# A decoder step in float32: scores, values and state products of the sample tokens on four column groups of TensorE instead of two

## The chip, the cores and the metric

One Trainium2 chip, one core of it. The metric is the device time of the kernel in microseconds (us), as the median of several runs. Before the change three runs took 1352.76, 1353.05 and 1354.18 us, so the median is 1353.05.

## What is computed

One inference step of a hybrid decoder layer, for a prompt of 1024 tokens and for 32 sample tokens (8 batches of 4). One input projection feeds three branches (a gated MLP, a Mamba-2 scan, a cross-attention to 256 memory tokens), one output projection joins them. The change touches the sample tokens alone, in two places. Each of the 8 batches has its own keys, values and scan state:

```python
y_off = jnp.einsum('bclgn,bcgkpn,bclgk->bclgkp', cm, h_prev, jnp.exp(acum))   # C times the state, 16 heads x 64
s = jnp.einsum('bthd,bmhd->bhtm', qh, mem_k) * (MEM_HEAD_DIM ** -0.5)         # 4 heads x 256
p = jax.nn.softmax(s, axis=-1)
o = jnp.einsum('bhtm,bmhd->bthd', p, mem_v)
```

## The kernel before

**The main line.** TensorE does large projections all the time. `gemmA` and `gemmB` run eight k-steps of three matmuls each (lines 290 to 292 in `gemm3`): the operands are split into a float32r part and its remainder. One call is a block; `spill` makes three blocks of 352 tokens from one weight unit, each block is evicted by ScalarE into a tile `gt` (line 701) and stored by a DMA on the SyncE queue (line 702, `mg_d<-gt` and the like).

**The side work.** The sample tokens are handled by a generator, `side_chain()`, stepped from `hook()` after each k-step. The pace is 0.43, so one step of the generator falls after every two or three k-steps, and a bare `yield` is a step without work that lets other engines finish. The generator runs `sample_scan` and then `sample_att` beside the projections; `side.drain()` runs what is left when the projections of that part are through. TensorE takes all of it in program order.

**Products with the states** (`sample_scan`, `s1` and `s2`). Per batch b: `s1` transposes the state (0.5 MB, tile `hb`, line 1027) into `hTb`; `s2(b, 0)` multiplies it by the masked C. The stationary operand has 32 columns, so the product uses 32 of the array's 128 columns. Group g of the heads goes to the column group that starts at column 32 g (`tile_position`), 512 columns of states streaming: two products per batch (line 1039), accumulated over the batches in one PSUM bank. After the last batch two copies of 32x512 take the sums out (line 1070).

**Scores** (`sample_att`). Keys come as 32 half tiles `kv` of 0.5 MB (16 of keys, 16 of values; half a holds heads 2a and 2a+1), five buffers. Per batch and half there is one step of eight transposes (line 1152, copied by ScalarE and VectorE into `kTb`, two buffers) and, one half later, one step of scores: two parts of the head dimension times two heads, four products of 32 stationary and 256 streaming columns, head h on column group h (line 1137). This makes 16 score steps.

**Values.** After the softmax the probabilities are spread into the mask tile `pm`. Per batch and half: a load of the half that comes four later (line 1117), and four products, two halves of the memory times two heads (line 1188). This makes 16 value steps.

**The queue.** All these DMAs are issued by SyncE in program order. A load of `kv` waits until TensorE has read the buffer that it overwrites; a store `mg_d<-gt` waits for ScalarE's eviction. What stands behind a waiting DMA waits too.

Of the kernel before, what the change touches and what calls it, by code (L numbers as in the profile page):

```python
# [58 lines left out]
def hybrid_step(ctx, tc, x_prompt, x_sample, mem_prompt, state_ssm, state_conv, cache_mem_k,  # L59
# [25 lines left out]
    # every float32 operand of the large products is split exactly into a float32r part (H) and  # L85
    # a float32r remainder (L); products are H*H + H*L + L*H, accumulated in float32
# [17 lines left out]
    def split(raw, H, L, heng, leng):  # L104
        """H = float32r(raw), L = raw - H"""
        if heng is ACT:
            ACT.activation(out=H, in_=raw, func=AF.Copy)  # L107
        else:
            heng.tensor_copy(out=H, in_=raw)
        leng.tensor_tensor(out=L, in0=raw, in1=rb(H), op=ALU.subtract)  # L110

# [114 lines left out]
    # 1 where the token belongs to the batch: 0 <= p - 4 b <= 3  # L226
# [17 lines left out]
    class RowNorm:  # L244
        """rows xt [T, 1024] -> dH + dL [128, 8, T] = (rmsnorm(xt) * g)^T"""
# [27 lines left out]
    # work that runs beside the large products: stepped between their parts  # L273
# [12 lines left out]
    def gemm3(ps, lhs, rhs, k0, kn, first, last, mid=None):  # L286
        """ps += sum over k of lhs(k)^T rhs(k) in three float32r products"""
        for k in range(k0, k0 + kn):
            (lH, lL), (rH, rL) = lhs(k), rhs(k)
            PE.matmul(out=ps, lhsT=lH, rhs=rH, start=(first and k == k0), stop=False)  # L290
            PE.matmul(out=ps, lhsT=lH, rhs=rL, start=False, stop=False)  # L291
            PE.matmul(out=ps, lhsT=lL, rhs=rH, start=False, stop=(last and k == k0 + kn - 1))  # L292
            if mid is not None and k == 3:
                mid()
            hook()
# [10 lines left out]
    def gemmA(w, mH, mL, t0, n):  # L306
        """weights stationary: [128 channels, n tokens]"""
        ps = mm()
        gemm3(ps[:, :n], lambda k: (w[0][:, k, :], w[1][:, k, :]),
              lambda k: (mH[:, k, t0:t0 + n], mL[:, k, t0:t0 + n]), 0, KD, True, True)  # L310
        w_tick()
        return ps

    def gemmS(wp, n, dst):
        """the 32 sample tokens stationary, H and L side by side: [dst = 32 tokens, n channels]; the weights
        are released"""
        ps = mm()
        for k in range(KD):
            wH, wL = wp[k // 4][0][:, k % 4, :], wp[k // 4][1][:, k % 4, :]
            if k > 0:  # L320
                PE.matmul(out=ps[:32, :n], lhsT=xS[:, k, 0:32], rhs=wL, start=False, stop=False)
            PE.matmul(out=ps[:64, :n], lhsT=xS[:, k, :], rhs=wH, start=(k == 0), stop=(k == KD - 1))
            if k == 0:
                PE.matmul(out=ps[:32, :n], lhsT=xS[:, k, 0:32], rhs=wL, start=False, stop=False)
            if k == 3:
                w_half()
            hook()
        w_done(1)
        ACT.activation(out=dst, in_=ps[:32, :n], func=AF.Copy)
        DVE.tensor_tensor(out=dst, in0=dst, in1=ps[32:64, :n], op=ALU.add)  # L330
        w_tick()

    def gemmB(mH, mL, t0, T, wp, n, last=False):
        """tokens stationary: [T tokens, n channels]; after the last tile the weights are released"""
        ps = mm()
        gemm3(ps[:T, :n], lambda k: (mH[:, k, t0:t0 + T], mL[:, k, t0:t0 + T]),
              lambda k: (wp[k // 4][0][:, k % 4, :], wp[k // 4][1][:, k % 4, :]), 0, KD, True, True,
              w_half if last else None)
        if last:
            w_done(1)  # L340
        w_tick()
        return ps

    # =====================================================================
    # Phase B: Mamba-2
    # =====================================================================
# [48 lines left out]
    # the activation table is loaded while the first rows arrive  # L395
# [15 lines left out]
    def setup_side():  # L411
# [5 lines left out]
        # conv state, transposed  # L417
# [7 lines left out]
        # rows of the decay products: rows 0-7 and 8-15 pick a head (1 on its columns), 16-17 hold  # L425
        # the running sums (H, L) of the chunk
# [52 lines left out]
    # parameter vectors, one 128-vector per row, then transposed  # L479
# [22 lines left out]
    def x_side(t):  # L502
        # beside the products of tile t: transposes of tile t + 1, norm of tile t + 2
# [31 lines left out]
    def dt_chain(pool):  # L535
# [10 lines left out]
        # log1p(e) = ln(u) * e / (u - 1), or e where u == 1  # L546
# [9 lines left out]
        # dta = -exp(a_log) * dt  # L556
# [53 lines left out]
    def chunk_rows(i0):  # L610
        """rows of chunk i % 8 of group i // 8, four of them"""
# [104 lines left out]
    def gate_norm(pool, y, sz, T):  # L716
        """y = y * sz; returns the scale to unit mean square; y, sz [T, 512]; sz is overwritten"""
# [29 lines left out]
    def lr_copy(i):  # L747
        """decay rows of chunks i .. i + 3"""
        if i < 16:
            DVE.tensor_copy(out=Lt, in_=Lraw)  # L750
            DVE.tensor_copy(out=Rt, in_=Rraw)
            if i + 4 < 16:
                chunk_rows(i + 4)
# [34 lines left out]
    def sC(i):  # L788
        """the chunk's C, for the product with the state"""
# [11 lines left out]
    def sE(i, j):  # L801
        """masked decays of four heads (transposed): exp(min(diff, 0))"""
# [137 lines left out]
    def sample_scan(sp2):  # L940
# [39 lines left out]
        # H, L, H of B against H, H, L of x: one pass over 96 rows  # L980
# [54 lines left out]
        def s2(b, j):  # L1035
            hbt, hTb, Bm = St[b]
            if j == 0:
                for g in range(2):
                    PE.matmul(out=accs[32 * g:32 * g + 32, :], lhsT=Cm[:, g, b * 32:(b + 1) * 32],
                              rhs=hTb[:, g * 512:(g + 1) * 512], start=(b == 0), stop=(b == 7), tile_position=(0, 32 * g))  # L1040
# [23 lines left out]
        for g in range(2):  # L1064
# [5 lines left out]
            DVE.tensor_copy(out=t1[:, cs], in_=accs[32 * g:32 * g + 32, :])  # L1070
# [21 lines left out]
    def softmax_rows(pool, ps, n):  # L1092
        """ps [128, n, 256] scores -> P [128, n, 256]"""
# [15 lines left out]
    def sample_att(sap):  # L1109
# [23 lines left out]
        def scores(b, a):  # L1133
            kTb = kTs.pop((b, a))
            for dt in range(2):
                for h in (2 * a, 2 * a + 1):
                    PE.matmul(out=psS[h * 32:(h + 1) * 32, :], lhsT=qm[:, 2 * h + dt, b * 32:(b + 1) * 32],
                              rhs=kTb[:, 2 * (h - 2 * a) + dt, :], start=(b == 0 and dt == 0), stop=(b == 7 and dt == 1),
                              tile_position=(0, h * 32))

        prev = None
        for b in range(8):
            for a in range(2):
                kv_load()
                kb = kvq.pop(0)
                kTb = sap.tile([128, 4, 256], F32, tag="kTb", name="kTb", bufs=2)
# [13 lines left out]
                if prev is not None:  # L1160
                    scores(*prev)
                    yield
                prev = (b, a)
        yield
        scores(*prev)
# [16 lines left out]
        for b in range(8):  # L1182
            for a in range(2):
                kv_load()
                vb = kvq.pop(0)
                for m in range(2):
                    for h in (2 * a, 2 * a + 1):
                        PE.matmul(out=psO[h * 32:(h + 1) * 32, :], lhsT=pm[:, m, h, b * 32:(b + 1) * 32],
                                  rhs=vb[:, m, (h - 2 * a) * 256:(h - 2 * a + 1) * 256], start=(b == 0 and m == 0),
                                  stop=(b == 7 and m == 1), tile_position=(0, h * 32))  # L1190
# [36 lines left out]
    # =====================================================================  # L1227
    # Phase A: spatial-gating MLP
    # =====================================================================
# [90 lines left out]
    def mix(h):  # L1320
        """mixes head h; the result takes the place of v: vt[:, c, h] = [channels, tokens of chunk c]"""
# [52 lines left out]
    TB = [(0, 384), (384, 384), (768, 288)]  # L1374

    def outproj(H, L, first, at=None):
        units = [(ct, b) for ct in range(8) for b in range(3)]
        if first:
            # the last tokens are split last
# [35 lines left out]
    def splitA(c, leng=DVE):  # L1415
        """all heads of token tile c"""
# [53 lines left out]
    # =====================================================================  # L1470
    # Phase C: memory cross-attention
    # =====================================================================
# [27 lines left out]
    n = 0  # L1500
# [140 lines left out]
    def y_load(i):  # L1641
        """summed output of the other branches: the block's tokens of one channel tile"""
# [23 lines left out]
    # the output weights stay: the first ones in the slots of the stream  # L1666
# [20 lines left out]
    def rows_part(b, ct):  # L1687
        """transposes of one channel tile back to token rows, plus the residual"""
# [15 lines left out]
        if ct in SQE:  # L1704
# [12 lines left out]
            # the gain, once the squares are taken  # L1717
# [91 lines left out]
```

## Time and profile before

| what | number |
|---|---|
| median of three runs | 1353.05 us |
| profiled execution, first to last instruction (its span) | 1351.7 us |
| TensorE busy (matmul) | 1320.8 us, 98% |
| VectorE, ScalarE, GpSimd busy | 590.4, 496.5, 210.4 us |
| scan of the sample tokens, its products with states | about 516 to 562 us of the span |
| scores of the sample tokens | about 590 to 655 us |
| values of the sample tokens | about 662 to 698 us |

The rows come from one profiled execution; its device time isn't listed by itself, so the span (1351.7) stands for it, 1.35 us below the median of the runs. In the profile, a float32 product of the sample tokens shows as two MATMUL records: 64 products of scores are 128 records. A float32r matmul, and a transpose, is one record. [...]

### The profile page before, as it was taken

Reading aid. Unit: us, or ns where it says so; the run is one execution under the profiler, and the core shown is the slowest. Engines: PE = TensorE matmul, PEld = TensorE weight load, DVE = VectorE, ACT = ScalarE, POOL = GpSimd, SP = SyncE. Lnnn points to the kernel's source line nnn. Section 1 sums busy time; section 2 is a strip of 40 time slices with the busy share of each in tenths; the row PEclk is TensorE's granted clock in tenths of the full one; section 3 lists DMA queues with packets and bytes.
Section 4 is the critical chain, followed back from the end, with each engine's and each line's share of the span. In section 5 each row is a group of like instructions: output and inputs, shape, how many; then the busy total and the mean of one; then the engine's idle time right before and its main releaser. Section 6 shows DMA issues by size and latency. Waiting matters only on the chain. (4 is left out here: it accounts for less than half of the span.)

```text
span 1351.7 us, 22582 instructions
## 1 busy us (share of the span) xinstructions
PE 1320.8 (98%) x9231; PEld 1236.4 (91%) x9231; DVE 590.4 (44%) x943; ACT 496.5 (37%) x962; POOL 210.4 (16%) x274
## 2 busy tenths in 40 slices
PE   8999999999999999999999999999999889999996
PEld 7999999988888898888779999998999889999996
DVE  6212545566767632422112245345312646654543
ACT  6323444464545432222211124344313633322322
POOL 4200000043434424200000010002000600000122
PEclk9999999999999999999999999999999999999999
DMA  6223111122222245475551114221423565436432
GB/s 223 78 77 99 44 48 48 47 88 76 78 72 88 82 118 165 149 226 179 181 181 45 32 32 127 68 68 44 144 93 128 177 178 182 151 117 193 139 121 95
DMA packets 171595, 151.44 MB, mean 112 GB/s; under 512 B 13781, under 2 KB 155049, under 8 KB 171493
## 3 DMA queue, kind: packets, MB, share of 16 engines
q1 hardware_dynamic: 171492, 150.01, 36.1%
q8 instruction: 72, 1.18, 0.4%
q14 instruction: 31, 0.25, 0.1%
HBM read 111.97 MB, written 37.79 MB: 111 GB/s over the span
## 5 line engine op out<-in xcount | busy, mean ns | idle before, releaser
L290 PE MATMUL ps_mm<-xH,wh 128*128 128x352 f32 x1056 | 359.9, 341 | 0.0
L292 PE MATMUL ps_mm<-xH,wl 128*128 128x352 f32 x1056 | 339.6, 322 | 0.0
L291 PE MATMUL ps_mm<-xL,wh 128*128 128x352 f32 x1056 | 339.2, 321 | 0.0
L290 PEld LDWEIGHTS ps_mm<-xH,wh 128*128 128x128 f32 x1056 | 198.3, 188 | 25.3 <-issue 21.0
L291 PEld LDWEIGHTS ps_mm<-xL,wh 128*128 128x128 f32 x1056 | 199.0, 188 | 0.7
L292 PEld LDWEIGHTS ps_mm<-xH,wl 128*128 128x128 f32 x1056 | 198.4, 188 | 0.0
L110 DVE TENSOR_TENSOR wl<-wr,wh 128x1024 fp32r<-128x1024 f32 (+2 forms) x106 | 121.8, 1161 | 175.2 <-ACT wh L107 174.8
L290 PE MATMUL ps_mm<-wh,xH 128*128 128x256 f32 (+1 forms) x512 | 148.0, 289 | 0.0
L291 PE MATMUL ps_mm<-wl,xH 128*128 128x256 f32 (+1 forms) x512 | 146.4, 286 | 0.1
L292 PE MATMUL ps_mm<-wh,xL 128*128 128x256 f32 (+1 forms) x512 | 145.6, 284 | 0.3 <-DVE xL L110 0.3
L107 ACT ACTIVATE wh<-wr 128x1024 fp32r<-128x1024 f32 (+3 forms) x113 | 101.7, 915 | 36.2 <-PE ps_mm L291 14.2
L292 PEld LDWEIGHTS ps_mm<-wh,xL 128*128 128x128 f32 x512 | 98.1, 192 | 0.6 <-DVE xL L110 0.5
L290 PEld LDWEIGHTS ps_mm<-wh,xH 128*128 128x128 f32 x512 | 97.8, 191 | 0.4
L291 PEld LDWEIGHTS ps_mm<-wl,xH 128*128 128x128 f32 x512 | 97.7, 191 | 0.4 <-POOL wl L110 0.4
L701 ACT ACTIVATE gt<-ps_mm 128x352 f32<-128x352 f32 x72 | 33.0, 458 | 98.2 <-PE ps_mm L292 77.1
L290 PE MATMUL ps_mm<-aH,wh 128*128 128x384 f32 (+1 forms) x192 | 62.7, 327 | 1.9 <-ACT gt L1403 1.0
L290 PE MATMUL ps_mm<-bH,wh 128*128 128x384 f32 (+1 forms) x192 | 64.0, 334 | 0.0
L291 PE MATMUL ps_mm<-aL,wh 128*128 128x384 f32 (+1 forms) x192 | 63.0, 328 | 0.3
L292 PE MATMUL ps_mm<-bH,wl 128*128 128x384 f32 (+1 forms) x192 | 62.4, 325 | 0.2 <-DVE wl L110 0.2
L291 PE MATMUL ps_mm<-bL,wh 128*128 128x384 f32 (+1 forms) x192 | 62.5, 326 | 0.0
L292 PE MATMUL ps_mm<-aH,wl 128*128 128x384 f32 (+1 forms) x192 | 61.9, 323 | 0.0
L1720 POOL TENSOR_TENSOR xres<-xres,gfin 128x1536 f32<-128x1536 f32 (+3 forms) x6 | 14.4, 2392 | 231.6 <-ACT junk L1714 231.6
(385 smaller groups left out, 2472.8 us busy)
## 6 DMA issues: line engine op xcount, KB each, us to landing
wr<-in_w_in_dram SPq DMA_DIRECT2D x60, 512.0 KB
wr<-in_w_out_dram SPq DMA_DIRECT2D x24, 512.0 KB
kv<-in_cache_mem_k_dram SPq DMA_DIRECT2D x16, 512.0 KB
kv<-in_cache_mem_v_dram SPq DMA_DIRECT2D x16, 512.0 KB
y_d<-gt SPq DMA_DIRECT2D x32, 192.0 KB
q_d<-gt SPq DMA_DIRECT2D x24, 176.0 KB
gg_d<-gt SPq DMA_DIRECT2D x24, 176.0 KB
mg_d<-gt SPq DMA_DIRECT2D x24, 176.0 KB
```

Source lines behind the costliest of these rows:

```text
L107: ACT.activation(out=H, in_=raw, func=AF.Copy)
L110: leng.tensor_tensor(out=L, in0=raw, in1=rb(H), op=ALU.subtract)
L290: PE.matmul(out=ps, lhsT=lH, rhs=rH, start=(first and k == k0), stop=False)
L291: PE.matmul(out=ps, lhsT=lH, rhs=rL, start=False, stop=False)
L292: PE.matmul(out=ps, lhsT=lL, rhs=rH, start=False, stop=(last and k == k0 + kn - 1))
L701: ACT.activation(out=t[:, :BLK], in_=ps[:, :BLK], func=func)
L1720: eng.tensor_tensor(out=t[:, 0:nf, c0:c0 + w], in0=t[:, 0:nf, c0:c0 + w], in1=gc.unsqueeze(1).to_broadcast([128, nf, w]), op=ALU.mult)
```

## The change

Three edits. The products with the states are cut into four pieces of 256 columns, one on each column group. The scores of both halves of a batch are made in one step, eight products, the four heads in turn; the step comes after the transposes of the next batch's first half, and `kTb` has three buffers. The values of a batch are made in one step of eight products that takes both halves, followed by two loads, the second of them one step of the generator later. (The diff also drops comments and docstrings; that part is left out here. Line numbers move by two in `sample_att`: scores are line 1139, loads 1119, transposes 1153, values 1186.)

```diff
@@ sample_scan, s2 @@
-                for g in range(2):
-                    PE.matmul(out=accs[32 * g:32 * g + 32, :], lhsT=Cm[:, g, b * 32:(b + 1) * 32],
-                              rhs=hTb[:, g * 512:(g + 1) * 512], start=(b == 0), stop=(b == 7), tile_position=(0, 32 * g))
+                for q in range(4):
+                    PE.matmul(out=accs[32 * q:32 * q + 32, 0:256], lhsT=Cm[:, q // 2, b * 32:(b + 1) * 32],
+                              rhs=hTb[:, q * 256:(q + 1) * 256], start=(b == 0), stop=(b == 7), tile_position=(0, 32 * q))
@@ sample_scan, end @@
-            DVE.tensor_copy(out=t1[:, cs], in_=accs[32 * g:32 * g + 32, :])
+            for e in range(2):
+                q = 2 * g + e
+                DVE.tensor_copy(out=t1[:, q * 256:(q + 1) * 256], in_=accs[32 * q:32 * q + 32, 0:256])
@@ sample_att, scores @@
-        def scores(b, a):
-            kTb = kTs.pop((b, a))
+        def scores(b):
+            kT = [kTs.pop((b, a)) for a in range(2)]
             for dt in range(2):
-                for h in (2 * a, 2 * a + 1):
+                for h in range(4):
                     PE.matmul(out=psS[h * 32:(h + 1) * 32, :], lhsT=qm[:, 2 * h + dt, b * 32:(b + 1) * 32],
-                              rhs=kTb[:, 2 * (h - 2 * a) + dt, :], start=(b == 0 and dt == 0), stop=(b == 7 and dt == 1),
+                              rhs=kT[h // 2][:, 2 * (h % 2) + dt, :], start=(b == 0 and dt == 0), stop=(b == 7 and dt == 1),
                               tile_position=(0, h * 32))
 ...
-                kTb = sap.tile([128, 4, 256], F32, tag="kTb", name="kTb", bufs=2)
+                kTb = sap.tile([128, 4, 256], F32, tag="kTb", name="kTb", bufs=3)
 ...
-                if prev is not None:
-                    scores(*prev)
+                if b and not a:
+                    scores(b - 1)
                     yield
-                prev = (b, a)
         yield
-        scores(*prev)
+        scores(7)
@@ sample_att, values @@
         for b in range(8):
-            for a in range(2):
+            vb = [kvq.pop(0) for _ in range(2)]
+            for m in range(2):
+                for h in range(4):
+                    PE.matmul(out=psO[h * 32:(h + 1) * 32, :], lhsT=pm[:, m, h, b * 32:(b + 1) * 32],
+                              rhs=vb[h // 2][:, m, (h % 2) * 256:(h % 2 + 1) * 256], start=(b == 0 and m == 0),
+                              stop=(b == 7 and m == 1), tile_position=(0, h * 32))
+            for _ in range(2):
                 kv_load()
-                vb = kvq.pop(0)
-                for m in range(2):
-                    for h in (2 * a, 2 * a + 1):
-                        PE.matmul(out=psO[h * 32:(h + 1) * 32, :], lhsT=pm[:, m, h, b * 32:(b + 1) * 32],
-                                  rhs=vb[:, m, (h - 2 * a) * 256:(h - 2 * a + 1) * 256], start=(b == 0 and m == 0),
-                                  stop=(b == 7 and m == 1), tile_position=(0, h * 32))
                 yield
```

How the order of instructions moves, at three places.

TensorE, the products with the states of one batch (`ps_acc` the accumulating bank, `hTb` the transposed state, `Cm` the masked C), as a piece of the difference:

```order
 L291 MATMUL ps_mm<-xL,wh 128x352
 L292 MATMUL ps_mm<-xH,wl 128x352
-L1039 MATMUL ps_acc<-hTb,Cm 32x512 x2
+L1039 MATMUL ps_acc<-hTb,Cm 32x256 x4
 L1044 MATMUL ps_sd<-Bm,X_5363 128x128 x4
 L290 MATMUL ps_mm<-xH,wh 128x352
```

Two products of 512 columns have become four of 256 at the same place; the rows around them stay.

TensorE, one step of the values before, the first half of batch 2 (`kv` a half tile of values, `pm` the masked probabilities):

```order
L292 MATMUL ps_mm_6937<-xH_74,wl_6618 128x352
L1188 MATMUL ps_acc_6903<-kv_6904,pm_6865 32x256 x4
L290 MATMUL ps_mm_6937<-xH_74,wh_6617 128x352
L291 MATMUL ps_mm_6937<-xL_75,wh_6617 128x352
L292 MATMUL ps_mm_6937<-xH_74,wl_6618 128x352
```

And now, the whole of batch 2:

```order
L292 MATMUL ps_mm_6905<-xH_74,wl_6466 128x352
L1186 MATMUL ps_acc_6856<-kv_6865,pm_6808 32x256 x2
L1186 MATMUL ps_acc_6856<-kv_6876,pm_6808 32x256 x2
L1186 MATMUL ps_acc_6856<-kv_6865,pm_6808 32x256 x2
L1186 MATMUL ps_acc_6856<-kv_6876,pm_6808 32x256 x2
L290 MATMUL ps_mm_6905<-xH_74,wh_6465 128x352
L291 MATMUL ps_mm_6905<-xL_75,wh_6465 128x352
L292 MATMUL ps_mm_6905<-xH_74,wl_6466 128x352
```

Four products of two heads have become eight of four heads, from two half tiles. Between two such steps there were two or three k-steps before; now there are 5, 5, 4, 5, 5, 4 and 5, which makes 33 over the eight steps. The scores moved in the same manner: eight steps of eight products, and between them the transposes of two halves.

SyncE, the loads of values from the fifth on (`kv_6904` the fifth, with `wr` the next weights and `mg_d` the stores of the gate), before:

```order
L702 DMA mg_d_80<-gt_6887 128x352
L1117 DMA kv_6904<-in_cache_mem_v_dram 128x2x512
L1117 DMA kv_6916<-in_cache_mem_v_dram 128x2x512
L169 DMA wr_6932<-in_w_in_dram 128x4x256
L702 DMA mg_d_80<-gt_6934 128x352
L1117 DMA kv_6941<-in_cache_mem_v_dram 128x2x512
L1117 DMA kv_6953<-in_cache_mem_v_dram 128x2x512
L1117 DMA kv_6965<-in_cache_mem_v_dram 128x2x512
L1117 DMA kv_6980<-in_cache_mem_v_dram 128x2x512
L702 DMA mg_d_80<-gt_6986 128x352
L1117 DMA kv_6996<-in_cache_mem_v_dram 128x2x512
L1117 DMA kv_7008<-in_cache_mem_v_dram 128x2x512
```

And now, again from the fifth (`kv_6865`) on:

```order
L702 DMA mg_d_80<-gt_6849 128x352
L1119 DMA kv_6865<-in_cache_mem_v_dram 128x2x512
L1119 DMA kv_6876<-in_cache_mem_v_dram 128x2x512
L1119 DMA kv_6892<-in_cache_mem_v_dram 128x2x512
L1119 DMA kv_6900<-in_cache_mem_v_dram 128x2x512
L702 DMA mg_d_80<-gt_6902 128x352
L1119 DMA kv_6923<-in_cache_mem_v_dram 128x2x512
L1119 DMA kv_6931<-in_cache_mem_v_dram 128x2x512
L1119 DMA kv_6947<-in_cache_mem_v_dram 128x2x512
L702 DMA mg_d_80<-gt_6952 128x352
L1119 DMA kv_6962<-in_cache_mem_v_dram 128x2x512
L1119 DMA kv_6978<-in_cache_mem_v_dram 128x2x512
```

The same loads stand closer together, with fewer stores and weights between them; the twelfth half tile (`kv_6962`) stands directly behind a store.

## Rows read from the trace of the kernel before

**Rows 1.** The page's first part: busy time, share of the span and instructions of each engine.

```profile
PE 1320.8 (98%) x9231; PEld 1236.4 (91%) x9231; DVE 590.4 (44%) x943; ACT 496.5 (37%) x962; POOL 210.4 (16%) x274
```

**Rows 2.** The view by windows: products with states, scores, values. Columns: stretch, its length, busy time and instructions of PE, PEld, DVE, ACT and POOL, granted clock, DMA share, GB/s.

```profile
515.00:562.00 47.00, 46.05 (x295) 37.24 (x295) 12.60 (x17) 11.07 (x21) 19.70 (x14) 1.00 0.66 193
590.00:656.00 66.00, 66.00 (x460) 52.44 (x459) 14.23 (x20) 15.28 (x27) 0.72 (x1) 1.00 0.55 174
662.00:698.00 36.00, 36.00 (x237) 22.78 (x235) 2.48 (x3) 2.80 (x5) 0.00 (x0) 1.00 0.70 228
```

**Rows 3.** The waits of TensorE over the whole span, the longest and the only one in these stages (us in total, times, longest).

```profile
PE ps_sd L270 <- DVE xn L262: 4.6, 4, 1.8
...
PE ps_sd L1027 <- DMA hb<-in_state_ssm_dram: 1.0, 1, 1.0
```

**Rows 4.** Groups of instructions by line, 515 to 700 us: scores, values, products with states (busy us, mean ns of one, idle before).

```profile
L1137 PE MATMUL ps_acc<-kTb,qm 128*32 128x256 f32 x128 | 16.9, 385 | 0.0
L1188 PE MATMUL ps_acc<-kv,pm 128*32 128x256 f32 x128 | 16.9, 385 | 0.0
...
L1039 PE MATMUL ps_acc<-hTb,Cm 128*32 128x512 f32 x32 | 8.4, 604 | 0.0
```

**Rows 5.** The timeline of TensorE around two steps of scores (heads 0 and 1, then heads 2 and 3) and the transposes between them. Columns: start, length, engine, line, what, count of records.

```profile
590.20 0.32 PE L292 MATMUL ps_mm<-xH,wl 128*128 128x352 f32 x1
590.45 1.06 PE L1137 MATMUL ps_acc<-kTb,qm 128*32 128x256 f32 x8
591.43 0.43 PE L290 MATMUL ps_mm<-xH,wh 128*128 128x352 f32 x1
...
592.34 0.32 PE L292 MATMUL ps_mm<-xH,wl 128*128 128x352 f32 x1
592.50 0.32 PE L290 MATMUL ps_mm<-xH,wh 128*128 128x352 f32 x1
592.66 0.32 PE L291 MATMUL ps_mm<-xL,wh 128*128 128x352 f32 x1
592.82 0.33 PE L292 MATMUL ps_mm<-xH,wl 128*128 128x352 f32 x1
592.98 1.04 PE L1152 MATMUL ps_sd<-ident,kv 128*128 128x128 f32 x8
...
594.65 0.32 PE L292 MATMUL ps_mm<-xH,wl 128*128 128x352 f32 x1
594.91 1.06 PE L1137 MATMUL ps_acc<-kTb,qm 128*32 128x256 f32 x8
595.90 0.43 PE L290 MATMUL ps_mm<-xH,wh 128*128 128x352 f32 x1
```

**Rows 6.** The timeline of TensorE around two float32 products of 32 stationary columns that stand alone: one of 512 streaming columns, one of 256.

```profile
505.14 1.04 PE L1001 MATMUL ps_sd<-Rs,Ls 17*32 17x512 f32 x2
506.11 0.43 PE L290 MATMUL ps_mm<-xH,wh 128*128 128x352 f32 x1
...
759.29 0.61 PE L1279 MATMUL ps_sd<-w,rep 4*32 4x256 f32 x2
759.84 0.30 PE L321 MATMUL ps_mm<-wl,xS 128*32 128x256 f32 x1
```

**Rows 7.** The timeline of TensorE around the first products with states, and at the transposes of the third batch's state.

```profile
515.89 1.05 PE L1039 MATMUL ps_acc<-hTb,Cm 128*32 128x512 f32 x4
516.87 0.66 PE L1044 MATMUL ps_sd<-Bm,X 96*128 96x128 f32 x4
...
520.91 1.06 PE L1027 MATMUL ps_sd<-ident,hb 128*128 128x128 f32 x8 [0.95 <-DMA hb<-in_state_ssm_dram]
```

**Rows 8.** The timeline of TensorE around the first steps of values.

```profile
661.93 0.32 PE L292 MATMUL ps_mm<-xH,wl 128*128 128x352 f32 x1
662.18 1.06 PE L1188 MATMUL ps_acc<-kv,pm 128*32 128x256 f32 x8
663.17 0.43 PE L290 MATMUL ps_mm<-xH,wh 128*128 128x352 f32 x1
```

**Rows 9.** What the loads take. The timeline of SyncE and ScalarE at the start (a load of 0.5 MB and its first reader), of SyncE at the loads of two states, and the view by windows of TensorE's line 1137 around 590 us (last two columns: DMA share, GB/s).

```profile
1.20 0.36 SPq L383 DMA_DIRECT2D xt<-in_x_prompt_dram  x1
4.98 1.06 ACT L256 ACTIVATE xn<-xt 128x1024 f32<-128x1024 f32 x1 [2.69 <-DMA xt<-in_x_prompt_dram]
...
514.20 1.44 SPq L937 DMA_DIRECT2D hb<-in_state_ssm_dram  x2
...
590.20:590.45 0.25, 0.00 (x1) 0.01 (x1) 1.00 1.04 393
590.45:590.68 0.23, 0.23 (x2) 0.14 (x4) 1.00 1.07 401
```

**Rows 10.** The softmax between scores and values: the timeline of GpSimd, VectorE and TensorE.

```profile
655.28 2.02 POOL L1170 MEMSET pm<- 128x2304 f32 x1 [73.90 <-PE ps_acc L1137]
657.98 0.35 DVE L1104 TENSOR_SCALAR P<-P,sm 128x256 f32<-128x256 f32 x1
659.49 0.38 PE L1175 MATMUL ps_sd<-ident,P 128*128 128x128 f32 x2
659.97 0.49 DVE L1177 COPY pm<-ps_sd 128x128 f32<-128x128 f32 x2 [1.64 <-PE ps_sd L1175]
```

**Rows 11.** The timeline of VectorE after the last products with states, and the view by windows at the first stretch of a lower clock (columns as in group 2).

```profile
562.61 0.67 DVE L1070 COPY t_s<-ps_acc 32x512 f32<-32x512 f32 x1
...
744.25:747.66 3.41, 3.41 (x18) 3.41 (x17) 0.00 (x0) 0.00 (x0) 0.00 (x0) 0.50 0.00 0
747.66:751.00 3.34, 3.34 (x30) 3.34 (x29) 0.43 (x1) 0.77 (x2) 0.00 (x0) 1.00 0.00 0
```

More of the change, by code (lines that the diff above doesn't have):

```diff
@@ L1131, in sample_att @@
         kTs = {}
-        def scores(b, a):
-            kTb = kTs.pop((b, a))
+        def scores(b):
+            kT = [kTs.pop((b, a)) for a in range(2)]
             for dt in range(2):
-                for h in (2 * a, 2 * a + 1):
+                for h in range(4):
                     PE.matmul(out=psS[h * 32:(h + 1) * 32, :], lhsT=qm[:, 2 * h + dt, b * 32:(b + 1) * 32],
-                              rhs=kTb[:, 2 * (h - 2 * a) + dt, :], start=(b == 0 and dt == 0), stop=(b == 7 and dt == 1),
+                              rhs=kT[h // 2][:, 2 * (h % 2) + dt, :], start=(b == 0 and dt == 0), stop=(b == 7 and dt == 1),
                               tile_position=(0, h * 32))
-        prev = None
         for b in range(8):
```

## The prediction

> **What bounds the kernel now.** I read the page's first part, then the windows of the three stages that the change touches, then TensorE's waits, then its timeline step by step. TensorE is busy for 98% of the span [rows 1]. In the scores and the values it is busy without a gap, 66.00 of 66.00 and 36.00 of 36.00 us; in the products with states it lacks 0.95 of 47.00 [rows 2], and that is one wait for a load of a state [rows 3]. VectorE, ScalarE and GpSimd are busy for less than half of each stage. So in these stages TensorE's own work sets the end: what the side work takes off TensorE comes off the span, unless something is late in its place.
>
> How full is TensorE in that work? The mean of 385 ns of a record [rows 4] doesn't tell, since records overlap; starts do. One float32 product of 32 stationary and 512 streaming columns, alone, takes 506.11 - 505.14 = 0.97 us until the next matmul starts, and one of 256 takes 759.84 - 759.29 = 0.55 [rows 6]. So 256 streaming columns cost 0.42, and 0.13 is paid once. Now two products of 512 columns on two column groups: 516.87 - 515.89 = 0.98 [rows 7], as much as one alone. And four products of 256 on two column groups: 591.43 - 590.45 = 0.98 [rows 5] = 0.13 + 2 x 0.42. **The two column groups run at the same time; a step costs what its longest column group costs.** Half of the array's column groups stand idle in each of these steps.
>
> **The sum.** A k-step of the main line is three matmuls 0.16 apart (592.34, 592.50, 592.66, 592.82 in [rows 5]), 0.48.
>
> *Scores.* A step costs the main line the time between the matmuls around it, less the 0.16 that they are apart anyway: 591.43 - 590.20 - 0.16 = 1.07, of which 0.09 is getting in. There are 16 steps: 17.1 us. Afterwards there are 8, with four column groups of two products each: 0.09 + 0.98, and 0.01 for two more starts (my estimate, from the pairs, whose second product adds 0.01 to a product alone: 0.98 against 0.97): 1.08, in all 8.6. Saved: **8.5**.
>
> *Values.* 663.17 - 661.93 - 0.16 = 1.08 [rows 8], 16 times is 17.3; then 8 times 1.08, 8.6. Saved: **8.7**.
>
> *States.* Now 0.98 a batch; with 256 columns on each group one product's time, 0.55. 0.43 x 8 = 3.4. But the third batch's transposes wait for their load [rows 7]: TensorE comes there 0.43 sooner and waits 1.38 instead of 0.95. Saved: **3.0**.
>
> *At nothing.* The number of transposes and matmuls of the main line stays; eight steps of the generator fall away, so by the order of instructions the side work ends 19 k-steps earlier, beside blocks that run anyway. VectorE's two copies of 32x512 (0.67 each, [rows 11]) become four of 32x256, at least 0.34 and at most 0.67 each, so up to 1.3 us more on an engine with five empty steps of the generator behind it; if that cover were gone, the last transposes of the scan would come 1.3 later. The third buffer of `kTb` is read two steps after it is written, and the copies into it are on engines with over 75% idle time [rows 2]. The softmax: the transposes of P come 10 k-steps after the last scores instead of 9, and P was ready 1.2 us early (658.33 against 659.49); the first values come 4 k-steps after them instead of 5, and `pm` was ready at 660.46 against 662.18, 1.7 early [rows 8, 10]. Losing one k-step leaves 1.2. Keys: a batch now takes seven k-steps, two steps of transposes and one of scores, 7 x 0.48 + 2 x 0.79 + 1.08 = 6.0 us for two loads, 1.05 MB or 175 GB/s beside weights and stores, and a load is issued four halves (12 us) ahead. No wait.
>
> *The values' loads* are the one new risk. Eight batches with 33 k-steps between them come every 33 / 7 x 0.48 + 1.08 = 3.3 us instead of one half every 2.2. Two halves of 0.52 MB in 3.3 us, with a store and a part of the weights, are some 370 GB/s at worst against 393 to 401 that the DMA engines moved when full [rows 9]: just enough. The lead: the second half that a batch needs is loaded into the buffer that the batch two before gives back, so it's issued 1.0 us after that batch begins and has 2 x 3.3 - 1.0 = 5.6 us. The trace shows a load of that size from issue to its reader in 3.8 us with little beside it (1.20 to 4.98) and in 6.7 among stores (514.20 to 520.91) [rows 7, 9]. At 3.8 nothing waits. At 6.7 the first batch that needs one waits 1.1, and from there the time between batches is at least (6.7 + 1.0) / 2 = 3.85, 0.5 more, five times; with the load that stands behind a store, about 5 us in all. I take **1.0**: the stream is of reads, at most two are issued together, so it is nearer to 3.8; but the twelfth half stands behind a store that waits for its eviction, and has a lead of only about 4.2 (an estimate: one k-step, eviction and issue add some 1.4 to the 1.0).
>
> Sum: 8.5 + 8.7 + 3.0 - 1.0 = 19.2. The span of 1351.7 becomes 1332.5. The median of the runs is 1353.05, 1.35 above that span, and I leave this difference as it is: 1333.9, **1334 us**.
>
> **The rivals.**
>
> *Two column groups at a time.* The trace has no more than two narrow products on their own column groups at once. If four products on four groups took turns in pairs, a step of scores would be 0.09 + 0.13 + 4 x 0.42 = 1.90 against two of 1.07, saving 0.24 x 8 = 1.9, the values 2.0, the states nothing: 3.9, **1349 us**. For it: nothing but the lack of evidence. Against it: groups 2 and 3 pair just like 0 and 1, 595.90 - 594.65 - 0.16 = 1.09 against 1.07 [rows 5], so each of the four groups has its own way in, and nothing is seen to be shared by a pair. [...] Chance 6%.
>
> *The loads of the values become the bound.* If two halves came no faster than the stage's mean now, 228 GB/s [rows 2], a batch would need 1.05 / 0.228 = 4.6 us, 1.3 more than 3.3, seven times 9 us of waiting instead of 1: **1342 us**. For it: this is the only stage whose demand grows by half. Against it: 228 is what was asked for, not what the engines can do, which was 400 in short stretches. Chance 10%.
>
> *Slower: the groups shut one another out.* If more than two streams of float32 at once made each product run alone (one reading port, one bank written by four), a step of scores would be 0.22 + 8 x 0.42 = 3.58, eight of them 28.6 against 17.1; values 11.3 more, states 0.13 + 4 x 0.42 - 0.98 = 0.83 more, 6.6 in all: **1382 us**. It decides from the point where a step of eight products costs over 2.15, twice the present one; that is 4.6 products in a row instead of 2. Against it: two groups write the same bank today and lose 0.01. Chance 3%.
>
> **How the numbers follow.** My forecast has 79%: 1334, with 1330 to 1339 for its own unknowns (no wait for values, or 5 us of it). One stretch of lower clock more or less moves it by about 1.3 us: in 3.41 us at a granted clock of 0.50 TensorE did 18 matmuls where the next 3.34 us had 30 [rows 11]; the three stages here all ran at 1.00. The late loads (1342) have 10%, pairs (1349) 6%, slower (1382) 3%, what I have not thought of 2%. The range is 1330 to 1344: it takes in the first two cases and leaves some 13% out. 0.2% is 2.7 us, about what a measurement of this kernel can tell. Faster by more than that is all of the first three cases but a little: 93%. Within: 3%. Slower: 4%.
>
> **What the profile will show.** Right: scores and values as 128 records each in 8 bursts of 16; from the burst's first start to the next matmul 1.0 us; the states' products as 64 records, 0.55 to 0.58 from the first to line 1044; a wait of about 1.4 at the transposes of the third state; TensorE waiting for `kv` 0 to 5 us in all. Wrong: a burst of 1.8 us or more (pairs, or worse), values more than 5 us behind their loads, or a wait in the scores, the softmax or after the scan that wasn't there.

## The result and the profile after

The changed kernel takes 1330.19 us (median of four runs, 1329.36 to 1334.83), the kernel before 1352.9 on the same chip (1352.70 to 1354.18). The ratio is 0.9838, with a 95% interval of 0.9817 to 0.9858: 22.7 us, or 1.7%, come off. The forecast was 1334 with 1330 to 1344. The profiled execution took 1329.36, with a span of 1327.6 against 1351.7.

First the page's part 1 of the changed kernel, then its windows of the three stages, then the groups by line, which answer to [rows 1, 2, 4].

```profile
PE 1297.0 (98%) x9263; PEld 1228.8 (93%) x9263; DVE 588.7 (44%) x945; ACT 496.4 (37%) x962; POOL 209.0 (16%) x274
```

```profile
514.00:558.00 44.00, 42.55 (x326) 37.16 (x325) 12.59 (x17) 11.34 (x21) 19.95 (x15) 1.00 0.69 200
583.00:633.00 50.00, 50.00 (x423) 43.31 (x422) 13.44 (x18) 14.33 (x25) 0.00 (x0) 1.00 0.73 234
640.00:668.00 28.00, 26.80 (x227) 19.45 (x227) 1.26 (x2) 3.09 (x6) 0.00 (x0) 1.00 0.88 296
```

```profile
L1186 PE MATMUL ps_acc<-kv,pm 128*32 128x256 f32 x128 | 10.5, 386 | 1.2 <-DMA kv<-in_cache_mem_v_dram 1.2
...
L1139 PE MATMUL ps_acc<-kTb,qm 128*32 128x256 f32 x128 | 8.6, 385 | 0.0
L1039 PE MATMUL ps_acc<-hTb,Cm 128*32 128x256 f32 x64 | 5.1, 391 | 0.0
```

The work is the same (128 records of scores, 128 of values), the mean of a record is the same, 385 or 386 ns, and the time in which any of them runs has halved: 16.9 to 8.6 in the scores. So twice as many run at once. Only the values have gaps, 1.2 us, and the DMA share there has gone from 0.70 to 0.88.

One step shows it, in TensorE's timeline around the scores of one batch in the changed kernel:

```profile
588.98 0.32 PE L292 MATMUL ps_mm<-xH,wl 128*128 128x352 f32 x1
589.22 1.07 PE L1139 MATMUL ps_acc<-kTb,qm 128*32 128x256 f32 x16
590.22 0.43 PE L290 MATMUL ps_mm<-xH,wh 128*128 128x352 f32 x1
590.49 0.32 PE L291 MATMUL ps_mm<-xL,wh 128*128 128x352 f32 x1
```

Sixteen records (eight products) keep the main line away for 590.22 - 589.22 = 1.00 us; eight records took 0.98 in [rows 5]. The states, in the same view: the first products of a batch, and the late transposes of the third.

```profile
515.16 0.64 PE L1039 MATMUL ps_acc<-hTb,Cm 128*32 128x256 f32 x8
515.73 0.66 PE L1044 MATMUL ps_sd<-Bm,X 96*128 96x128 f32 x4
...
520.27 0.95 PE L1027 MATMUL ps_sd<-ident,hb 128*128 128x128 f32 x7 [1.45 <-DMA hb<-in_state_ssm_dram]
```

0.57 from the products to the next matmul where [rows 7] had 0.98, and 1.45 of waiting for the load where it had 0.95.

The values, again in TensorE's timeline, the first, third and eighth batch:

```profile
640.14 1.07 PE L1186 MATMUL ps_acc<-kv,pm 128*32 128x256 f32 x16
641.14 0.43 PE L290 MATMUL ps_mm<-xH,wh 128*128 128x352 f32 x1
...
647.32 0.63 PE L1186 MATMUL ps_acc<-kv,pm 128*32 128x256 f32 x4
648.27 1.06 PE L1186 MATMUL ps_acc<-kv,pm 128*32 128x256 f32 x12 [0.33 <-DMA kv<-in_cache_mem_v_dram]
649.26 0.43 PE L290 MATMUL ps_mm<-xH,wh 128*128 128x352 f32 x1
...
665.85 0.32 PE L292 MATMUL ps_mm<-xH,wl 128*128 128x352 f32 x1
666.17 0.63 PE L1186 MATMUL ps_acc<-kv,pm 128*32 128x256 f32 x4
667.49 1.06 PE L1186 MATMUL ps_acc<-kv,pm 128*32 128x256 f32 x12 [0.69 <-DMA kv<-in_cache_mem_v_dram]
668.48 0.43 PE L290 MATMUL ps_mm<-xH,wh 128*128 128x352 f32 x1
```

A batch on time costs 1.00. In a late one, the first four records (heads 0 and 1) start, the other twelve wait for the second half tile, and the twelve alone take 0.99: the early start saves nothing. So the third batch costs 649.26 - 647.32 = 1.94, of which 0.94 is delay, although the idle time shown is 0.33. **Idle time understates a late operand where a part of the burst covers it.** The fourth, seventh and eighth batch lose 0.06, 0.79 and 1.38 in the same way: 3.2 us in all, where TensorE's waits, the next two lines, put 1.2 down to `kv`.

```profile
PE ps_sd L1027 <- DMA hb<-in_state_ssm_dram: 1.4, 1, 1.4
...
PE ps_acc L1186 <- DMA kv<-in_cache_mem_v_dram: 1.2, 3, 0.7
```

Why they are late stands in SyncE's timeline and in the windows (last two columns: DMA share and GB/s), both of the changed kernel:

```profile
640.54 0.46 SPq L702 DMA_DIRECT2D mg_d<-gt  x1
641.09 4.11 SPq L1119 DMA_DIRECT2D kv<-in_cache_mem_v_dram  x4
646.53 0.34 SPq L702 DMA_DIRECT2D mg_d<-gt  x1
646.96 2.89 SPq L1119 DMA_DIRECT2D kv<-in_cache_mem_v_dram  x3
653.77 0.34 SPq L702 DMA_DIRECT2D mg_d<-gt  x1
654.20 2.30 SPq L1119 DMA_DIRECT2D kv<-in_cache_mem_v_dram  x3
656.59 0.42 SPq L169 DMA_DIRECT2D wr<-in_w_in_dram  x1
658.78 0.34 SPq L702 DMA_DIRECT2D mg_d<-gt  x1
659.21 1.22 SPq L1119 DMA_DIRECT2D kv<-in_cache_mem_v_dram  x2
```

```profile
642.00:644.00 2.00, 2.00 (x20) 1.70 (x22) 0.00 (x0) 0.00 (x0) 0.00 (x0) 1.00 0.98 328
...
646.00:648.00 2.00, 1.94 (x13) 1.24 (x11) 0.00 (x0) 0.46 (x1) 0.00 (x0) 1.00 1.06 388
...
652.00:654.00 2.00, 2.00 (x21) 1.59 (x13) 0.00 (x0) 0.72 (x2) 0.00 (x0) 1.00 1.00 365
```

Halves five to eight are issued within 4.1 us, behind a store, and the DMA engines are full from 642 to 654: in six windows of 2 us their share is 0.98 to 1.06 at 328 to 389 GB/s. The sixth half, issued second of the four at 641.57, is read 6.7 us later, at 648.27; the last pair, issued at 659.21 and 659.71, is read at 666.17 and 667.49, 7.0 and 7.8 later. From 636 to 668 the queue itself stood 18.4 us at stores that waited for ScalarE's eviction (five times, 6.2 the longest) and 5.3 at loads of `kv` that waited for TensorE (four times, 2.2 the longest).

The softmax, which lost one k-step of its cover, didn't hold TensorE up (timeline of the changed kernel; it answers to [rows 10]):

```profile
637.93 0.38 PE L1175 MATMUL ps_sd<-ident,P 128*128 128x128 f32 x2
638.41 0.49 DVE L1177 COPY pm<-ps_sd 128x128 f32<-128x128 f32 x2 [1.81 <-PE ps_sd L1175]
640.14 0.37 PEld L1186 LDWEIGHTS ps_acc<-kv,pm 128*32 128x32 f32 x12 [0.21 <-issue]
```

`pm` is ready at 638.9, 1.2 before the first values, as forecast.

### The profile page after: what moved, and what is told of

It reads as the page before. It is cut to its first block, busy times and chain, and to the rows that moved or that the text cites. A ratio compares the mean times of both kernels' runs of the same rounds, so it can differ in the third digit from the quotient of the medians.

```text
span 1327.6 us, 22644 instructions
## 1 busy us (share of the span) xinstructions
PE 1297.0 (98%) x9263; PEld 1228.8 (93%) x9263; DVE 588.7 (44%) x945; ACT 496.4 (37%) x962; POOL 209.0 (16%) x274
```

## The experiments

Whole times differ by several us from run to run of one and the same kernel (41 runs of the kernel before lie between 1350.09 and 1358.44), so the stages are compared too: from the start of one matmul of the main line to the start of another, the same two in every kernel (among the matmuls that write `ps_mm`, in their order: the states from the 2641st to the 2833rd, scores and values from the 2941st to the 3361st; **behind** is the rest of the span). The next column adds up the stretches at a granted clock of 0.50 behind the stages, without the one at the span's very end. Each row is one profiled execution.

| kernel | states | scores and values | behind | at half clock behind | span |
|---|---|---|---|---|---|
| before | 59.94 | 119.19 | 648.4 | 13.6 | 1351.7 |
| changed | 57.13 | 103.45 | 643.6 | 6.8 | 1327.6 |
| states alone | 57.22 | 119.19 | 646.8 | 10.2 | 1347.9 |
| scores alone | 60.21 | 109.72 | 649.7 | 13.7 | 1344.8 |
| values alone | 60.33 | 112.95 | 650.5 | 13.7 | 1348.8 |
| six buffers | 57.14 | 100.62 | 650.4 | 13.6 | 1332.0 |
| changed again | 57.11 | 104.73 | 650.2 | 13.7 | 1336.4 |
| early load | 57.21 | 102.56 | 648.8 | 6.8 | 1332.9 |
| two heads, then two | 57.23 | 104.18 | 646.6 | 10.2 | 1331.8 |
| head after head | 57.32 | 104.46 | 645.6 | 3.4 | 1331.2 |
| changed, third time | 57.22 | 104.45 | 645.2 | 10.2 | 1329.9 |
| six buffers again | 57.26 | 100.80 | 646.0 | 10.2 | 1328.6 |
| seven buffers | 57.28 | 100.25 | 642.1 | 3.4 | 1323.2 |

### The parts alone

**States alone**, the two hunks of `sample_scan`:

```diff
-                for g in range(2):
-                    PE.matmul(out=accs[32 * g:32 * g + 32, :], ...
+                for q in range(4):
+                    PE.matmul(out=accs[32 * q:32 * q + 32, 0:256], ...
```

> The kernel before with the products with the states alone in four pieces. Theory 1 (a step costs what its longest column group costs): from the first product to line 1044 0.57 us instead of 0.98, eight times, less 0.42 that the third state's load takes back: 2.9 us less, about 1350.0 us. Theory 2 (a good part of the gain comes from the stretch after the sample tokens, which happened to be shorter): the same in the stage, but the stretch from the first 256-column matmul of the next phase to the end, 648.4 us before and 643.6 in the changed kernel, moves by up to 5 us with any shift: 1345 to 1350.

Measured: 1350.01 (10 runs, 1347.16 to 1354.79), ratio 0.9982 (0.9967 to 0.9997). The stage is 2.7 shorter.

**Scores alone**, the hunks of the scores with the third `kTb`:

```diff
-            for dt in range(2):
-                for h in (2 * a, 2 * a + 1):
+            for dt in range(2):
+                for h in range(4):
```

> The kernel before with the scores alone in eight steps of four heads. Theory 1: eight steps fewer; each cost 1.07 up to the next matmul and 0.11 more until the matmuls run 0.16 apart again, so 8 x 1.18 = 9.4 us less, about 1343.5 us. By the sum as predicted (1.07 a step, no more) 8.5 less, 1344.4. Theory 2: the stretch after the sample tokens is again shorter or not by up to 5 us whatever the steps save: 1338 to 1344.

Measured: 1345.48 (4 runs, 1344.23 to 1346.53), ratio 0.9943 (0.9922 to 0.9964). Scores and values are 9.47 shorter.

**Values alone**, the last hunk:

```diff
-            for a in range(2):
-                kv_load()
-                vb = kvq.pop(0)
+            vb = [kvq.pop(0) for _ in range(2)]
 ...
+            for _ in range(2):
+                kv_load()
```

> The kernel before with the values alone in eight steps of four heads. Theory 1: 9.4 us less from eight steps fewer, and the waits for the halves that the changed kernel showed, 3.2 us, come back: 6.2 less, about 1346.7 us. If the waits were an accident of where weights and stores stood in the queue: 9.4 less, 1343.5. Theory 2: up to 5 us less again from the stretch behind.

Measured: 1348.23 (10 runs, 1344.58 to 1350.75), ratio 0.9958 (0.9945 to 0.9972); 6.24 shorter, with 1.3 us of waits for `kv`.

What follows: the parts add up in their stages. 9.47 + 6.24 = 15.71 against 119.19 - 103.45 = 15.74 for both, and 2.7 against 2.8 for the states. No part pays for another. That the first sum agrees to 0.03 is luck, because the late loads differ from profile to profile: the changed kernel's later profiles have 104.73 and 104.45 in this stage. Without late loads it closes as well: with seven buffers (below) 119.19 - 100.25 = 18.94, twice the 9.47 of the scores alone. The whole times add up less well: the parts take 3.3 + 7.8 + 5.1 = 16.1 us off the median, less than their stages, and the changed kernel 20.7 to 22.7 in its three sets of runs, more than its stages.

### The late loads

**Six buffers** for keys and values:

```diff
-    KVB = 5
+    KVB = 6
```

> The changed kernel with six buffers for half tiles of keys and values instead of five, so that loads run five halves ahead. Theory 1: the fifth and sixth half of the values no longer stand behind the weights and the store at the start of the values, and each second half has one step more of lead; the 3.2 us of waits in the values fall to under 1: 2.5 to 3 us less than the changed kernel, 1327 to 1328 us. If the waits come from what the DMA engines can move and not from the lead: no change, 1330 us.

Measured: 1333.71 (4 runs, 1332.28 to 1337.28), ratio 0.986 (0.9836 to 0.9885). TensorE's waits have no `kv` any more, and the stage is 2.8 shorter than in the changed kernel, as expected. (The eighth batch still takes 1.37 us instead of 1.00; the part of the burst that could start hides the wait.) The whole time wasn't: 3.5 above the changed kernel's. The table says where it went: 650.4 behind the stages, where the program is the same, against 643.6.

So **the changed kernel again**, unchanged, with the early load beside it:

> The changed kernel once more, with more rounds. The three stages alone account for 2.8 + 9.5 + 6.2 = 18.5 us. Theory 1 (the stretch behind them has the same length on average, and varies from run to run by some us, as the kernel before does between 1350 and 1357): a median of 1334 to 1335 against the runs of before in the same job. Theory 2 (the changed kernel's later stretch is shorter every time): 1330 again, 22 to 23 us less than before.

Measured: 1332.28 (5 runs, 1329.48 to 1338.11), ratio 0.9838 (0.9824 to 0.9851). That is 21.3 less than before, between what the two theories said. The profiled run was the slowest, 1338.11, and had 650.2 behind the stages: with the same program 6.6 more than the first time, when the profiled run was the fastest of four. A single profile can't tell anything of that stretch.

**The fifth half earlier**, ahead of the softmax, since its buffer is free by then:

```diff
+        kv_load()
         P = softmax_rows(sap, psS.unsqueeze(1), 1)
```

> The changed kernel with the fifth half tile of values loaded one step earlier, right after the last scores and ahead of the weights and the store that stand before it now. Theory (the fifth and sixth half wait in the queue behind these two): the wait at the third batch of values, 0.9 us, goes, those at the seventh and eighth (0.8 and 1.4) stay: the stretch from the scores to the end of the sample tokens is 1 us shorter than in the changed kernel, 102.4 instead of 103.5. Rival (the DMA engines' rate is the limit): nothing there. In the whole time 1 us is hard to tell.

Measured: 1334.27 (4 runs, 1331.18 to 1335.89), ratio 0.9855 (0.984 to 0.987). The length of the stage fits, 102.56, but not the way to it: the seventh batch was to stay late, and its delay is gone with that of the third, while the eighth is late by 2.3 instead of 1.4, as TensorE's timeline of this kernel shows:

```profile
665.24 0.63 PE L1187 MATMUL ps_acc<-kv,pm 128*32 128x256 f32 x4
667.56 1.06 PE L1187 MATMUL ps_acc<-kv,pm 128*32 128x256 f32 x12 [1.70 <-DMA kv<-in_cache_mem_v_dram]
```

**Six buffers again, and seven** (`KVB = 7`), with the changed kernel a third time, all on one chip:

> The changed kernel once more, on the same chip as the two runs with more buffers. Nine runs of it so far lie between 1329.4 and 1338.1, with medians of 1330.2 and 1332.3. Both theories: median 1330 to 1334, waits of TensorE for kv near 3 us in three batches of the values, and a stretch behind the values that is 643 to 651 us long, by how many stretches of half clock it has.

> Six buffers for keys and values instead of five, once more. Theory 1 (the late loads cost 2.8 us in the values, and what comes behind only scatters): stage of the values 2.8 shorter than again2, and the median 1 to 4 us below again2's. Theory 2 (something behind the values takes the gain back each time, as in the first run, where the whole time was 3.5 above the changed kernel's): stage 2.8 shorter, median equal to again2's within 1 us or above it.

> Seven buffers. Theory 1: no wait for kv with six already, so the stage is as long as with six, and the median the same as kv6b's within 1 us, both below again2's. Theory 2: no lower than again2.

Measured: changed 1333.17 (4 runs, 1331.57 to 1336.20), ratio 0.9846 (0.9825 to 0.9868); six buffers 1329.20 (5 runs, 1325.04 to 1335.19), 0.9816 (0.9790 to 0.9842); seven 1330.31 (5 runs, 1324.95 to 1334.28), 0.9830 (0.9807 to 0.9852). The stage is 3.7 and 4.2 shorter than the changed kernel's on this chip. With seven, every batch of the values is on time, and the stage is 0.55 shorter than with six, where the fourth and the eighth batch were still 0.15 and 0.39 late; the expectation had no delay left with six. The third and the eighth, in TensorE's timeline, and then the window of the stretch in which the changed kernel was late:

```profile
647.64 1.07 PE L1186 MATMUL ps_acc<-kv,pm 128*32 128x256 f32 x16
648.64 0.43 PE L290 MATMUL ps_mm<-xH,wh 128*128 128x352 f32 x1
...
664.60 1.07 PE L1186 MATMUL ps_acc<-kv,pm 128*32 128x256 f32 x16
665.60 0.43 PE L290 MATMUL ps_mm<-xH,wh 128*128 128x352 f32 x1
```

```profile
642.00:654.00 12.00, 12.00 (x103) 9.60 (x102) 0.00 (x0) 1.88 (x3) 0.00 (x0) 1.00 1.00 362
```

The DMA engines are as full as before (share 1.00, 362 GB/s) and TensorE has no gap: what these eight batches lacked was lead, not bandwidth. That the stage gains 3 to 4 us is shown three times. On the whole time the medians are 3 to 4 below the changed kernel's on this chip, which speaks for the first theory; but the intervals overlap, and the first six-buffer run was above. Over all chips the changed kernel has a median of 1331.7 (13 runs), six and seven buffers 1331.2 (14 runs). Whether more buffers beat it as a whole is open.

### Does the order within a burst matter?

The change takes the four heads in turn. **Two heads, then two**, and **head after head**, eight products each as before, in scores and values:

```diff
-            for dt in range(2):
-                for h in range(4):
+            for dt, h in ((0, 0), (0, 1), (1, 0), (1, 1), (0, 2), (0, 3), (1, 2), (1, 3)):
```

```diff
-            for dt in range(2):
-                for h in range(4):
+            for h in range(4):
+                for dt in range(2):
```

> The changed kernel with the eight products of a step in another order: heads 0 and 1 with both their parts, then heads 2 and 3. If TensorE begins products in the order of the program, heads 2 and 3 begin when the second products of heads 0 and 1 have begun: three products in a row, 0.13 + 3 x 0.42 = 1.39 us from the first product to the next matmul. If each column group takes its own from the queue as soon as it is free: 0.99, as in the changed kernel. If only two groups can run at once: 1.81. Whole kernel 0, 6 or 13 us slower than the changed one.

> The changed kernel with the eight products of a step head after head, both products of a head next to each other. In the order of the program a head's second product waits for its first on the same columns, and the next head's first can begin with it: five products in a row, 0.13 + 5 x 0.42 = 2.23 us from the first product to the next matmul, 16 steps, some 20 us slower than the changed kernel, no better than the kernel before in the scores and the values. If each column group takes its own from the queue: 0.99 and no difference.

Measured: 1333.51 and 1333.03 (one run each). TensorE's timeline of the same step of scores, head after head:

```profile
589.51 0.32 PE L292 MATMUL ps_mm<-xH,wl 128*128 128x352 f32 x1
589.76 1.09 PE L1139 MATMUL ps_acc<-kTb,qm 128*32 128x256 f32 x16
590.78 0.43 PE L290 MATMUL ps_mm<-xH,wh 128*128 128x352 f32 x1
```

590.78 - 589.76 = 1.02, and 1.01 with two heads and then two: the expectation that a product waits for the one ahead of it in program order (2.23 and 1.39) failed. The starts of the single records in these traces show what holds instead: within a burst the four column groups begin 7 ns apart in turn, 13 ns head after head, which is 7 ns for each product that stands between them in the program. So TensorE here hands the products out in the order of the program, and one that finds its column group busy doesn't hold up those behind it. One whose operand is late does: in the late batches above, in turn, four records start before the wait, and head after head eight do. (A record doesn't name its head; this is read from distances and counts.) All four column groups fill in any of these orders, so "in turn" is worth 0.02 us a step at most, and the gain is in having all four heads in one step.

## Why the prediction was right, and where its sizes were off

**Four column groups at once: right.** This was the step on which all hung. A burst of 16 records takes 1.00 and not 1.90 (pairs in turn) or 3.58 (one after another); both rivals are out. Every burst of scores, and of values whose operands were there, took 1.00 or 1.01, which leaves no room for four products in a row either.

**States: right.** 0.57 a batch, 0.55 to 0.58 expected; the third state's wait 1.45, 1.38 expected. The three profiles with the old products have 60.2 on the mean and three of the changed kernel 57.2: 3.0, as forecast.

**A step's price: 0.11 too low.** I took the time between the matmuls around a step less the 0.16 that they are apart anyway. But the matmul after the step is itself slower to be followed. From the timeline of the kernel before, the one behind the step of [rows 5] at 591.43:

```profile
591.70 0.32 PE L291 MATMUL ps_mm<-xL,wh 128*128 128x352 f32 x1
```

591.70 - 591.43 = 0.27 instead of 0.16. So a step costs 1.18, and eight steps fewer are worth 9.4; the scores alone gave 9.47, where I had 8.5. Interrupting the main line has a price on both sides of the burst, here 0.09 ahead of it and 0.11 behind.

**The loads of the values: named, and mis-sized.** I took 1.0 us; it was 3.2, inside the 0 to 5 that the prediction allowed, and by the batches of its other two profiles 4.4 and 4.2. The failed step is "at most two are issued together, so it is nearer to 3.8". Four are issued in 4.1 us, and with full DMA engines a late one is read 6.7 to 7.8 after its issue: the upper price and more. For the first late half the prediction's other branch was right: at 6.7 it had 1.1 of waiting, and the third batch lost 0.94. The half that I suspected, the twelfth, cost nothing in the first profile; the sixth, fourteenth and sixteenth did. But in the second profile of the same program ("changed again") it was the worst. There its load was issued at 655.08, behind a store, and TensorE's timeline shows its batch, the sixth:

```profile
659.51 0.62 PE L1186 MATMUL ps_acc<-kv,pm 128*32 128x256 f32 x4
661.65 1.06 PE L1186 MATMUL ps_acc<-kv,pm 128*32 128x256 f32 x12 [1.52 <-DMA kv<-in_cache_mem_v_dram]
```

Its lead, 659.51 - 655.08 = 4.4, is what the prediction had (4.2); the load took 6.6, and the batch lost 2.1. Which half is late changes from run to run. Values in the first profile: 9.4 - 3.2 = 6.2, which is what the values alone gave, where I had 8.7 - 1.0 = 7.7. The rival in which the loads bind (9 us of waiting at 228 GB/s) is out: the DMA engines moved 328 to 389.

**The sum.** The two errors, scores 0.9 too low and values 1.5 too high, nearly cancel, which is luck: 3.0 + 9.4 + 6.2 = 18.6 against 19.2 forecast, and the stages of the first two profiles give 2.8 + 15.7 = 18.5. **The rest of the 24.1 between these two spans lies outside the change.** Behind the stages the changed kernel's first profile is 648.4 - 643.6 = 4.8 shorter, and ahead of them 0.7. This stretch has 642 to 651 us in 13 profiles, and two things in it vary: the time at half clock, 3.4 to 13.7 us (before 13.6, after 6.8), and TensorE's idle time between its instructions, 10.3 to 15.9 (12.5 and 11.1). Take the idle time and half of the time at half clock off, and 628.5 to 630.1 is left in all 13, with or without the change. So the program there costs the same, and a profile's length is a matter of how its waits and the clock fell. The early load had as little half clock as the changed kernel's first profile and was 5.2 longer, by its idle time. Much of the idle time is one tile. TensorE's waits for it, first line from the first profile of the changed kernel, second line from its second:

```profile
PE ps_mm L291 <- DVE wl L110: 1.6, 3, 1.1
PE ps_mm L291 <- DVE wl L110: 5.3, 5, 1.8
```

That the change itself brings anything there isn't shown: its own three profiles have 643.6, 645.2 and 650.2. The prediction had this scatter too small: it allowed for one stretch of lower clock more or less, 1.3 us (its own rows give 3.41 - 18 / 30 x 3.34 = 1.4), and for no change of the waits. By the medians of all runs, 1353.45 (41) and 1331.71 (13), the gain is 21.7. The stages explain 18.0 on the mean of the changed kernel's three profiles (3.0, and 119.19 - 104.21 = 15.0). How much of the other 3.7 is luck of the draw stays open.

**At nothing: right**, as far as a trace can show it. No wait appeared in the scores, the softmax or behind the scan.

## What to carry to other kernels

Narrow float32 products cost the time of the longest column group here (0.98 for four on two groups, 1.00 for eight on four), so fill all four in one step, and count what an interrupted main line loses ahead of the burst and behind it (0.09 and 0.11). When consumption is put into fewer, larger steps, look for the lead of a whole larger step more for its operands: with two more buffers, the two halves of a batch, all eight batches of values were on time. Look at what the DMA queue issues together (four halves in 4.1 us, late ones read 6.7 to 7.8 after their issue), not at the mean rate (228 GB/s before, [rows 2]). And compare stages between the same two instructions: whole times here scatter by as much as a part of the change is worth (13 runs of the changed kernel lie between 1329.36 and 1338.11; the values alone are worth 5.1).

## What the runs showed of the hardware that wasn't expected

**The same wait comes with the lower clock in one profile and without it in another.** TensorE waits at line 292 for `woL` in every profile. In the changed kernel's first profile (timeline, then window), the clock stays at 1.00:

```profile
1247.44 0.45 PE L292 MATMUL ps_mm<-cH,woL 128*128 128x384 f32 x1 [2.88 <-DVE woL L110]
```

```profile
1247.40:1251.00 3.60, 3.56 (x21) 3.55 (x22) 2.72 (x5) 0.76 (x3) 0.00 (x0) 1.00 0.50 133
```

In the second profile of the same program the same wait, longer by 0.04 us, is followed by 6.8 us at 0.50, with 20 matmuls in them:

```profile
1253.55 0.69 PE L292 MATMUL ps_mm<-cH,woL 128*128 128x384 f32 x1 [2.92 <-DVE woL L110]
```

```profile
1252.70:1259.50 6.80, 5.95 (x20) 5.87 (x21) 3.53 (x6) 1.86 (x7) 1.51 (x1) 0.50 0.50 158
```

In all 13 profiles this wait has 1.88 to 2.98 us. In seven of them, with waits from 2.09 up, a stretch of 3.4 or 6.8 us at 0.50 comes with it or right behind it; in six, with waits up to 2.88, none does. So the length of the wait alone doesn't decide it here. Of the 6.6 us by which these two profiles differ behind the stages, TensorE's idle time makes 3.4 and the lower clock about as much again.
